# The chunk rows of an SSD scan: a state product from split operands, and dt moved into the exponents

## The chip, the cores and the metric

The kernel runs on one core of a Trainium2 chip. The metric is the device time of one execution in microseconds, of which the median of three runs is given. The core's engines are TensorE (PE in the profile, with its weight loads as PEld), VectorE (DVE), ScalarE (ACT), GpSimd (POOL) and SyncE (SP, which here only starts transfers). Each works through its own queue in order, and they wait for one another with semaphores.

## The reference, cut to what matters

One inference step of a hybrid decoder layer: a pooling branch and a state-space branch side by side, merged by gates. 1024 rows of a prompt and 64 rows of samples go through it. The part that the change touches is the scan of the state-space branch over the prompt. It has 32 heads of 64 channels in 4 groups of 8, a state of 128 by 64 for each head, and goes over the rows in 8 chunks of 128. For each chunk the reference computes:

```
acs = cumsum(dq * A)                       # per row and head
decay[i, j] = exp(acs[i] - acs[j])         # i >= j, else 0
att = (C B^T)[i, j] * decay[i, j] * dq[j]
y = att @ x  +  C (exp(acs) * h)
w_in = exp(last - acs) * dq
h = h * exp(last)  +  B^T (w_in * x)
```

After it y gets d_skip * x added, is multiplied by silu(z), and goes through a norm and an output projection. All of it is float32.

## The kernel before, in words

The large products are done with operands split into two parts (a high part rounded to the type that the program calls F32R, and the rest as a low part), as three matmuls: high by high, high by low, low by high. Products of plain F32 operands go through TensorE in full precision, at more time for each column.

The stages follow one another: the input projection (up to some 480 us), the samples' scan woven into the last input products (to about 750 us), the prompt's chunks (about 757 to 1043 us), and the output products (to the end). `dt_end`, among the samples, makes the small tables that all chunks use: `dtT` (dt by row, chunk and head), `acT` (the running sum of dt times the positive rate, so that decays are exponentials of its negative), `wdT` (w_in) and `Elb` (exp(last)). It also writes the running sums to memory, from where `decays` loads them spread over all partitions.

A chunk, `chunk(g, c)` at L1492, is a generator in five steps, which the loop at L1844 takes at different times:

1. Loads, on SP: the running sums into `dec` (3 buffers), B and C into `bc`, and x into `xb` (5 buffers). Taken three chunks ahead.
2. ACT makes `cE`, the exponential of the running sums (L1504); POOL replaces what lies above the diagonal by a large number (L1229); ACT makes eight exponentials, one for each head, with the head's `acT` as bias (L1233). Two chunks ahead.
3. TensorE transposes x (L1511) and B (L1513) and multiplies B by C (L1514). ACT copies the transposed B to `bt` (L1516), and C into the same PSUM bank (L1518). DVE reads the transposed x from its bank twice: times dt into `xd` (L1522), and times w_in into `xw` (L1524, one buffer). DVE then multiplies `dec` and `cE` by the two products' rows (L1529, L1531). One chunk ahead.
4. TensorE makes the new state's product `pu` from `bt` and `xw` (L1536), and the heads' sums in `inner`: `xd` with `dec` (L1245) and the old state with `cE` (L1248). POOL lets the old state decay (L1542) and DVE adds `pu` (L1544) and d_skip * x (L1548).
5. `finish`, at L1462: times silu(z), which `load_sz` has loaded (3 buffers), split into high and low, and squares summed.

Between these steps the loop takes products of the pooling branch and of the chunks' results (`pieces`, whose matmuls are at L221), 2.56 pieces for each chunk, so that TensorE has work throughout. It also prepares the last products' weights (`wo_splits`, L1766).

What sets the order: over the chunk stage TensorE's and SP's instructions are held in the order in which the program writes them (`in_line`, L202, with ORDER at L1832). The instructions of ACT, DVE and POOL are put in order by the planner of the tile framework, which goes by its own simulated times. Two engines' uses of one PSUM tile are put one behind the other by the framework. PSUM tiles come from three sets: PA (three banks, the woven products), PB (four, with the transposes, the products of B and C, and the heads' sums taking turns) and PC (one, the state's product).

Of the kernel before, what the change touches and what calls it, by code (L numbers as in the profile page):

```python
# [8 lines left out]
F32 = mybir.dt.float32  # L9
F32R = mybir.dt.float32r  # L10
AF = mybir.ActivationFunctionType
ALU = mybir.AluOpType
# [8 lines left out]
P = 128  # L21
# [3 lines left out]
NB = 8  # L25
NS = 64
T = SEQ + NS
DI = 2048
NH = 32
# [4 lines left out]
NC = SEQ // CH  # L34
# [12 lines left out]
def tile_pool_ssd_step(  # L47
# [5 lines left out]
    nc = tc.nc  # L53
    uid = [0]

    def nm(s):
        uid[0] += 1
        return f"{s}_{uid[0]}"
# [25 lines left out]
    right = tc.tile_pool(name="tf", bufs=1, side="right", reuse_waits="tile")  # L84
# [8 lines left out]
    def Y4(pool, dt=F32R):  # L93
        return pool.tile([P, 4, T], dt, tag="Y", name=nm("Y"), bufs=2)

    def PB():
        return psB.tile([P, 512], F32, tag="ps", name=nm("ps"))
# [4 lines left out]
    def PC():  # L102

        return psC.tile([P, 512], F32, tag="pc", name=nm("pc"))
# [6 lines left out]
    mm = nc.tensor.matmul  # L111
    act = nc.scalar.activation
    V = nc.vector
# [990 lines left out]
    def dt_end():  # L1104
# [17 lines left out]
        def tmp(tag, bufs):  # L1122
            return sp.tile([P, 512], F32, tag=tag, name=nm(tag), bufs=bufs)[:, :F]
# [16 lines left out]
        r, e, p = tmp("xd", 2), tmp("xw", 1), tmp("hT", 1)  # L1140
# [18 lines left out]
        dt = dtT.rearrange("p c h -> p (c h)")  # L1159
# [20 lines left out]
        ac = acT.rearrange("p c h -> p (c h)")  # L1180
# [10 lines left out]
        for c0 in (8, 0, 4):  # L1191
            cs = range(c0, min(c0 + 4, 9))
            n = sum(P if c < 8 else NS for c in cs)
            ps = PB()
            for c in cs:
                m = P if c < 8 else NS
                nc.tensor.transpose(ps[:NH, (c - c0) * P:(c - c0) * P + m], acT[:m, c, :], ident[:m, :m])
            if c0 == NC:
                Es[0] = sp.tile([P, 2, 512], F32, tag="h0", name="E", bufs=H0B)[:NH, 0, :NS]
                V.tensor_copy(Es[0], ps[:NH, :n])  # L1200
                store_(acS_d.rearrange("b h t -> h b t"), Es[0].rearrange("h (b t) -> h b t", t=8))
            else:
                at = sp.tile([P, 512], F32, tag="xd", name=nm("at"), bufs=2)[:NH]
                V.tensor_copy(at[:, :n], ps[:NH, :n])
                store_(acs_d[c0:c0 + 4].rearrange("c h t -> h c t"), at.rearrange("h (c t) -> h c t", t=P))

    Es = [None, None]

# [14 lines left out]
    def decays(dec, g, c):  # L1223

        load(dec, acs_d[c, 8 * g:8 * g + 8, :].partition_broadcast(P))

    def far(dec, c):

        nc.gpsimd.affine_select(dec, dec, [[0, 8], [1, P]], ALU.is_ge, FAR, base=0, channel_multiplier=-1)  # L1229

    def exps(dec, g, c):
        for h in range(8):
            act(dec[:, h], dec[:, h], AF.Exp, bias=acT[:, c, 8 * g + h:8 * g + h + 1], scale=-1.0)  # L1233

    def load_E(E2, g):
        for hh in range(2):
# [3 lines left out]
    def inner(xd, dec, S, state=None, cE=None):  # L1240
        pi = PB()
        for q in range(4):
            o = [pi[64 * hh:64 * hh + 64, q * S:(q + 1) * S] for hh in range(2)]
            for hh in range(2):
                mm(o[hh], xd[:S, 2 * q + hh, :], dec[:S, 2 * q + hh], start=True, stop=state is None)  # L1245
            for hh in range(2 if state is not None else 0):
                h = 2 * q + hh
                mm(o[hh], state[:, h * 64:h * 64 + 64], cE[:, h], start=False, stop=True)  # L1248
        return pi[:, :4 * S].rearrange("p (q i) -> p q i", i=S)
# [205 lines left out]
    hst = [None] * NG  # L1455

    CKL = ("sz", "v")

    def ckt(shape, tag, bufs=2):
        return (cl if tag in CKL else ca if tag in ("dec", "xb", "cE", "bc") else ck).tile(list(shape), F32, tag=tag, name=nm(tag), bufs=bufs)  # L1460

    def finish(g, o, S, v, sz, y=None):  # L1462

# [21 lines left out]
    szs = []  # L1485

    def load_sz(j):
        g, c = divmod(j, NC)
        szs.append(ckt([P, 4, P], "sz", 3))
        load(szs[-1], z_d[g][:, :, c * P:c * P + P])  # L1490

    def chunk(g, c):  # L1492
        o = c * P
        dec = ckt([P, 8, P], "dec", 3)
        decays(dec, g, c)
        bc = ckt([P, 2, P], "bc", 3)
        load(bc, xbc_d[g][c][:, 4:6])
        Bf, Cf = bc[:, 0], bc[:, 1]
        xb = ckt([P, 4, P], "xb", 5)
        load(xb, xbc_d[g][c][:, 0:4])  # L1500
        yield
        if c > 0:
            cE = ckt([P, 8, P], "cE")
            act(cE, dec, AF.Exp, scale=-1.0)  # L1504
        if g > 0 or c > 0:
            far(dec, c)
            exps(dec, g, c)
            yield
        px = PB()
        for q in range(4):  # L1510
            nc.tensor.transpose(px[:, q * P:(q + 1) * P], xb[:, q], ident)  # L1511
        pbc = PB()
        nc.tensor.transpose(pbc[:, :P], Bf, ident)  # L1513
        mm(pbc[:, P:2 * P], Bf, Cf, start=True, stop=True)  # L1514
        bt = ckt([P, P], "bt", 2)
        act(bt, pbc[:, :P], AF.Copy)  # L1516
        if c > 0:
            act(pbc[:, 2 * P:3 * P], Cf, AF.Copy)  # L1518
        pxv = px.rearrange("p (h d) -> p h d", d=64)
        heads = slice(8 * g, 8 * g + 8)  # L1520
        xd = ckt([P, 8, 64], "xd", 2)
        V.tensor_tensor(xd, pxv, dtT[:, c, heads].unsqueeze(2).to_broadcast([P, 8, 64]), ALU.mult)  # L1522
        xw = ckt([P, 8, 64], "xw", 1)
        V.tensor_tensor(xw, pxv, wdT[:, c, heads].unsqueeze(2).to_broadcast([P, 8, 64]), ALU.mult)  # L1524
        if g == c == 0:
            yield
            far(dec, c)
            exps(dec, g, c)
        V.tensor_tensor(dec, dec, pbc[:, P:2 * P].unsqueeze(1).to_broadcast([P, 8, P]), ALU.mult)  # L1529
        if c > 0:  # L1530
            V.tensor_tensor(cE, cE, pbc[:, 2 * P:3 * P].unsqueeze(1).to_broadcast([P, 8, P]), ALU.mult)  # L1531
        yield
        if c == 0:
            yh[g], yl[g] = [Y4(hs if g % 2 else hp) for _ in range(2)]
        pu = PC()
        mm(pu, bt, xw.rearrange("p h d -> p (h d)"), start=True, stop=True)  # L1536
        pi = inner(xd, dec, P, *((hst[g], cE) if c > 0 else ()))
        hn = ckt([P, 512], "hst", 2)
        if c == 0:
            act(hn, pu, AF.Copy)  # L1540
        else:
            nc.gpsimd.tensor_tensor(hn.rearrange("p (h d) -> p h d", d=64), hst[g].rearrange("p (h d) -> p h d", d=64),  # L1542
                                    Elb[:, c, heads].unsqueeze(2).to_broadcast([P, 8, 64]), ALU.mult)
            V.tensor_tensor(hn, hn, pu, ALU.add)  # L1544
        hst[g] = hn

        for q in range(4):
            V.scalar_tensor_tensor(pi[:, q], xb[:, q], Dv[:, 4 * g + q:4 * g + q + 1], pi[:, q], ALU.mult, ALU.add)  # L1548
        yield
        finish(g, o, P, xb, szs.pop(0), pi)  # L1550
        if c == NC - 1:
            store_(new_ssm_p[g], hn)
# [55 lines left out]
        gas.append(right.__enter__())  # L1608

    def to_ssd():  # L1610
        nonlocal right, sd, sp, mask, maskS, blkS, dtT, acT, wdT, Elb, ElS
        right.__exit__(None, None, None)
        sd_cm = tc.tile_pool(name="sd", bufs=1, side="right", reuse_waits="tile")
        sd = sd_cm.__enter__()
        right_all.append(sd_cm)

        def one(shape, name):
            return sd.tile(shape, F32, tag=name, name=name, bufs=1)
        mask, maskS, blkS = one([P, P], "mask"), one([NS, NB, 8], "maskS"), one([NS, NS], "blkS")
        dtT, acT, wdT = one([P, 9, NH], "dtT"), one([P, 9, NH], "acT"), one([P, 9, NH], "wdT")  # L1620
        Elb, ElS = one([P, NC, NH], "Elb"), one([P, NB, NH], "ElS")
        right = tc.tile_pool(name="sp", bufs=2, side="right", reuse_waits="tile")
        sp = right.__enter__()
        dt_steps.append(dt_end())
        next(dt_steps[0])
    dt_steps = []
    right_all = []
    sd = sp = mask = maskS = blkS = dtT = acT = wdT = Elb = ElS = None

    first()  # L1630

# [55 lines left out]
    ca = None  # L1687
# [13 lines left out]
    cl = open_("cl", 2)  # L1701
    right = tc.tile_pool(name="ck", bufs=2, side="right", reuse_waits="tile")
    ck = right.__enter__()
    for shape, tag, bufs in (((P, 512), "ph", 3), ((P, P), "bt", 2), ((P, 8, 64), "xd", 2), ((P, 8, 64), "xw", 1),
                             ((P, 4, NS), "szs", 1), ((P, 512), "t2", 1), ((P, 512), "hst", 2)):
        ckt(shape, tag, bufs)

    sq_acc = hs.tile([P, T], F32, tag="sq", name="sq_acc", bufs=1)
# [127 lines left out]
    for _ in range(FRONT - 1):  # L1836
        next(pc_)
    next(seq[0])
    load_sz(0)
    next(seq[1])  # L1840
    next(pc_)
# [271 lines left out]
    for half in range(2):  # L2113
        c = slice(half * 512, half * 512 + 512)
# [168 lines left out]
```

## Time and profile before

| | us |
|---|---|
| three runs, median (lowest to highest) | 1214.07 (1212.27 to 1215.41) |
| the profiled execution | 1210.91 |
| its span | 1209.2 |
| busy: PE | 1194.4 |
| busy: PEld | 1118.5 |
| busy: DVE | 924.8 |
| busy: POOL | 763.4 |
| busy: ACT | 649.1 |

The span reaches from the first to the last instruction of the profiled execution. "Busy" is the time in which an engine had at least one instruction in work; a matmul's duration holds the time until its results are out, so that following matmuls overlap, and what one costs is read from start to start. A row of a group gives the line, the engine, the operation, the tiles (what is written, then what is read), the shapes and the count; behind the first bar the busy time in us and the mean duration in ns; behind the second the idle time of the engine just before, and what it had waited for. Idle time of an engine other than the one that sets the end costs nothing in itself.

### The profile page before, as it was taken

How to read it: one execution, taken by the hardware profiler on the slowest of the kernel's cores; microseconds unless marked ns; L12 is line 12 of the kernel's file. 1: busy time of each engine (PE TensorE's matmuls, PEld its weight loads, DVE VectorE, ACT ScalarE, POOL GpSimd, SP SyncE). 2: the span in 40 equal slices, each digit the busy share in tenths (PEclk: the TensorE clock that was granted, in tenths of full speed). 3: DMA queues.
4: the chain of work that ended last, by engine and by line, in shares of the span. 5: the costliest groups of instructions: out<-in, count | busy, mean ns of one | idle time of the engine just before them, and what ended most of it. 6: DMA issues, size and time to landing. Idle time of an engine off the chain costs nothing.

```text
span 1209.2 us, 25239 instructions
## 1 busy us (share of the span) xinstructions
PE 1194.4 (99%) x9242; PEld 1118.5 (93%) x9242; DVE 924.8 (76%) x1535; ACT 649.1 (54%) x1479; POOL 763.4 (63%) x655
## 2 busy tenths in 40 slices
PE   9999999999999999999999999999999999999997
PEld 8879999999999999999989999988888888999885
DVE  6993788877989578877576555687878889679976
ACT  6864356565666557454434334566676657312435
POOL 1137878875988787764777776255767758423653
PEclk9999999999999999999999999999999999999999
DMA  9836445574556455454667767988879888585794
GB/s 352 306 132 219 136 144 184 164 228 146 171 174 198 160 164 172 135 169 131 208 227 238 245 223 247 320 309 262 270 250 294 277 284 285 173 326 166 235 212 154
DMA packets 167924, 262.72 MB, mean 217 GB/s; under 512 B 32880, under 2 KB 80760, under 8 KB 167800
## 3 DMA queue, kind: packets, MB, share of 16 engines
q1 hardware_dynamic: 90408, 166.01, 41.9%
q10 hardware_dynamic: 73232, 87.16, 21.2%
q0 software_dynamic: 4160, 7.94, 3.2%
q8 instruction: 73, 1.20, 0.4%
q14 instruction: 51, 0.42, 0.1%
HBM read 173.31 MB, written 87.73 MB: 216 GB/s over the span
## 4 chain that ended last, share of the span: by engine, by line
PE 87%; DVE 5%; DMA 3%; ACT 2%; issue 1%; POOL 0%; ACTq 0%; DVEq 0%; SPq 0%; POOLq 0%
PE mm L411 24%; PE ps L411 23%; PE mm L221 17%; PE pc L411 5%; PE ps L1245 3%; PE pc L1536 2%; PE ps L1248 2%; PE ps L2036 2%; PE ps L2034 2%; PE ps L2035 2%; PE ps L1511 1%; DMA dec<-acs_d 1%; DMA Y<-in_x_prompt 1%; PE ps L957 1%; DVE tf L643 1%
## 5 line engine op out<-in xcount | busy, mean ns | idle before, releaser
L148 POOL TENSOR_TENSOR wlo<-rawA,whi 128x512 fp32r<-128x512 f32 x120 | 174.7, 1461 | 80.7 <-ACT whi L145 79.4
L221 PE MATMUL mm<-Y,whi 128*128 128x352 f32 (+1 forms) x960 | 195.9, 334 | 0.8 <-DVE G L1969 0.6
L148 POOL TENSOR_TENSOR wlo<-raw,whi 128x512 fp32r<-128x512 f32 x90 | 149.8, 1673 | 64.6 <-ACT whi L145 62.2
L221 PEld LDWEIGHTS mm<-Y,whi 128*128 128x128 f32 x960 | 159.2, 188 | 7.6 <-issue 4.1
L1089 DVE SCALAR_TENSOR_TENSOR GA<-GA,cvT,GA 128x1112 f32<-128x1112 f32 x72 | 134.0, 1866 | 0.1
L411 PE MATMUL mm<-Y,whi 128*128 128x272 f32 x800 | 118.4, 290 | 0.0
L145 ACT ACTIVATE whi<-rawA 128x512 fp32r<-128x512 f32 x120 | 75.1, 627 | 79.6 <-PE ps L411 34.7
L411 PE MATMUL ps<-Y,whi 128*128 128x272 f32 x800 | 117.4, 289 | 0.0
L145 ACT ACTIVATE whi<-raw 128x512 fp32r<-128x512 f32 x90 | 56.0, 629 | 103.9 <-DVE raw L348 34.0
L411 PEld LDWEIGHTS mm<-Y,whi 128*128 128x128 f32 x800 | 106.9, 188 | 2.5 <-issue 1.0
L411 PEld LDWEIGHTS ps<-Y,whi 128*128 128x128 f32 x800 | 107.0, 188 | 0.8 <-issue 0.7
L221 PE MATMUL mm<-Y,wlo 128*128 128x352 f32 (+1 forms) x480 | 98.5, 327 | 0.0
L1233 ACT ACTIVATE dec<-dec,acT 128x128 f32<-128x128 f32 x256 | 78.8, 389 | 25.8 <-POOL dec L1229 25.8
L221 PEld LDWEIGHTS mm<-Y,wlo 128*128 128x128 f32 x480 | 81.7, 188 | 0.0
L286 POOL TENSOR_TENSOR pw<-pw,ph 128x512 fp32r<-128x512 f32 x40 | 67.0, 1675 | 13.4 <-ACT ph L284 12.5
L1468 POOL TENSOR_TENSOR Y<-xb,Y 128x512 fp32r<-128x512 f32 x32 | 41.2, 1287 | 53.7 <-ACT Y L1466 53.7
L411 PE MATMUL mm<-G,whi 128*128 128x272 f32 x480 | 71.2, 290 | 0.0
L411 PE MATMUL ps<-G,whi 128*128 128x272 f32 x480 | 70.3, 289 | 0.0
L411 PE MATMUL mm<-Y,wlo 128*128 128x272 f32 x400 | 66.8, 288 | 0.0
L411 PE MATMUL ps<-Y,wlo 128*128 128x272 f32 x400 | 66.6, 288 | 0.0
L411 PEld LDWEIGHTS mm<-G,whi 128*128 128x128 f32 x480 | 64.1, 188 | 1.2 <-issue 1.1
L411 PEld LDWEIGHTS ps<-G,whi 128*128 128x128 f32 x480 | 64.2, 188 | 0.3 <-issue 0.3
(579 smaller groups left out, 3130.5 us busy)
## 6 DMA issues: line engine op xcount, KB each, us to landing
rawA<-in_w_in SPq DMA_DIRECT2D x62, 512.0 KB
dec<-acs_d SPq DMA_DIRECT2D x32, 512.0 KB
xbc<-GA ACTq DMA_DIRECT2D x24, 512.0 KB
Y<-wo SPq DMA_DIRECT2D x10, 1024.0 KB
pw<-in_w_ssm_out ACTq DMA_DIRECT2D x32, 256.0 KB
ws<-ph ACTq DMA_DIRECT2D x32, 256.0 KB
ws<-pw ACTq DMA_DIRECT2D x32, 256.0 KB
h<-in_state_ssm SPq DMA_DIRECT2D x32, 256.0 KB
```

Of the source, the lines that this page charges most:

```text
L145: ins = act(hi[:, :, :ncols], raw[:, :, :ncols], AF.Copy)
L148: (eng or nc.gpsimd).tensor_tensor(lo[:, :, :ncols], raw[:, :, :ncols], hi[:, :, :ncols].bitcast(F32), ALU.subtract)
L221: mm(ps[:, :n], w[k // 4][h][:, k % 4, :], r[k][:, o:o + n], start=(j == 0), stop=(j == len(terms) - 1))
L286: nc.gpsimd.tensor_tensor(raw.bitcast(F32R), raw, hi.bitcast(F32), ALU.subtract)
L411: mm(p, w[j // 8][:, k], A(k, s)[j // 4 == 1], start=(j == 0), stop=(j == 11))
L1089: V.scalar_tensor_tensor(d[:, :n], rp[:, k:k + n], cvT[:, 24 * k + mc:24 * k + mc + 1], d[:, :n], ALU.mult, ALU.add)
L1233: act(dec[:, h], dec[:, h], AF.Exp, bias=acT[:, c, 8 * g + h:8 * g + h + 1], scale=-1.0)
L1245: mm(o[hh], xd[:S, 2 * q + hh, :], dec[:S, 2 * q + hh], start=True, stop=state is None)
L1248: mm(o[hh], state[:, h * 64:h * 64 + 64], cE[:, h], start=False, stop=True)
L1468: nc.gpsimd.tensor_tensor(yl[g][:, :, o:o + S], v, yhc.bitcast(F32), ALU.subtract)
L1536: mm(pu, bt, xw.rearrange("p h d -> p (h d)"), start=True, stop=True)
L2034: mm(ps, hi, y[:, k, c0:c0 + cw], start=(first and k == 0), stop=False)
```

## The change

Four things are changed, all in the prompt's chunks or for them.

The state's product is made from split operands. `bt` becomes a pair, its first half rounded by ACT, its second half the rest, by DVE from PSUM. `xw` is split into `xh`, by ACT, and `xl`, by POOL, each with two buffers. Three matmuls add up in `pu` in place of the one in full precision.

dt goes into the exponents. `dt_end` makes a new table `alT` = ln(max(dt, 1e-37)) + running sum, for the chunks. The eight exponentials take it as bias in place of `acT`, so that the decays come out multiplied by dt. `xd` is then the transposed x as it is, and ACT copies it from PSUM; before, DVE multiplied it there.

There are more buffers: four for `sz`, six for `xb`.

The order of the tiles in the pool that opens for the chunks is another, with `xh` and `xl` among them, and the copy of C into PSUM (L1518 before) is written behind the two readings of the transposed x.

```diff
+        al = alT.rearrange("p c h -> p (c h)")
+        V.tensor_scalar(al, dt[:, :256], 1e-37, None, ALU.max)
+        act(al, al, AF.Ln)
+        V.tensor_tensor(al, al, ac[:, :256], ALU.add)
...
-            act(dec[:, h], dec[:, h], AF.Exp, bias=acT[:, c, 8 * g + h:8 * g + h + 1], scale=-1.0)
+            act(dec[:, h], dec[:, h], AF.Exp, bias=alT[:, c, 8 * g + h:8 * g + h + 1], scale=-1.0)
...
-        szs.append(ckt([P, 4, P], "sz", 3))
+        szs.append(ckt([P, 4, P], "sz", 4))
...
-        xb = ckt([P, 4, P], "xb", 5)
+        xb = ckt([P, 4, P], "xb", 6)
...
-        bt = ckt([P, P], "bt", 2)
-        act(bt, pbc[:, :P], AF.Copy)
-        if c > 0:
-            act(pbc[:, 2 * P:3 * P], Cf, AF.Copy)
+        bt = ckt([P, 2, P], "bt", 2, F32R)
+        act(bt[:, 0], pbc[:, :P], AF.Copy)
...
-        V.tensor_tensor(xd, pxv, dtT[:, c, heads].unsqueeze(2).to_broadcast([P, 8, 64]), ALU.mult)
-        xw = ckt([P, 8, 64], "xw", 1)
-        V.tensor_tensor(xw, pxv, wdT[:, c, heads].unsqueeze(2).to_broadcast([P, 8, 64]), ALU.mult)
+        act(xd, pxv, AF.Copy)
+        xw, xh, xl = ckt([P, 512], "xw", 1), ckt([P, 512], "xh", 2, F32R), ckt([P, 512], "xl", 2, F32R)
+        V.tensor_tensor(xw.rearrange("p (h d) -> p h d", d=64), pxv,
+                        wdT[:, c, heads].unsqueeze(2).to_broadcast([P, 8, 64]), ALU.mult)
+        if c > 0:
+            act(pbc[:, 2 * P:3 * P], Cf, AF.Copy)
+        act(xh, xw, AF.Copy)
+        nc.gpsimd.tensor_tensor(xl, xw, xh.bitcast(F32), ALU.subtract)
...
+        V.tensor_tensor(bt[:, 1], pbc[:, :P], bt[:, 0].bitcast(F32), ALU.subtract)
...
-        mm(pu, bt, xw.rearrange("p h d -> p (h d)"), start=True, stop=True)
+        mm(pu, bt[:, 0], xh, start=True, stop=False)
+        mm(pu, bt[:, 1], xh, start=False, stop=False)
+        mm(pu, bt[:, 0], xl, start=False, stop=True)
...
-    for shape, tag, bufs in (((P, 512), "ph", 3), ((P, P), "bt", 2), ((P, 8, 64), "xd", 2), ((P, 8, 64), "xw", 1),
-                             ((P, 4, NS), "szs", 1), ((P, 512), "t2", 1), ((P, 512), "hst", 2)):
+    for shape, tag, bufs in (((P, 8, 64), "xd", 2), ((P, 2, P), "bt", 2), ((P, 512), "ph", 3), ((P, 4, NS), "szs", 1), ((P, 512), "t2", 1),
+                             ((P, 512), "hst", 2), ((P, 512), "xw", 1), ((P, 512), "xh", 2), ((P, 512), "xl", 2)):
```

More of the change, by code (lines that the diff above doesn't have):

```diff
@@ L1457, in tile_pool_ssd_step, with ckt @@
     CKL = ("sz", "v")
-    def ckt(shape, tag, bufs=2):
-        return (cl if tag in CKL else ca if tag in ("dec", "xb", "cE", "bc") else ck).tile(list(shape), F32, tag=tag, name=nm(tag), bufs=bufs)
+    def ckt(shape, tag, bufs=2, dt=F32):
+        return (cl if tag in CKL else ca if tag in ("dec", "xb", "cE", "bc") else ck).tile(list(shape), dt, tag=tag, name=nm(tag), bufs=bufs)
     def finish(g, o, S, v, sz, y=None):
@@ L1610, in to_ssd @@
     def to_ssd():
-        nonlocal right, sd, sp, mask, maskS, blkS, dtT, acT, wdT, Elb, ElS
+        nonlocal right, sd, sp, mask, maskS, blkS, dtT, acT, wdT, alT, Elb, ElS
         right.__exit__(None, None, None)
@@ L1620, in to_ssd @@
         dtT, acT, wdT = one([P, 9, NH], "dtT"), one([P, 9, NH], "acT"), one([P, 9, NH], "wdT")
-        Elb, ElS = one([P, NC, NH], "Elb"), one([P, NB, NH], "ElS")
+        alT, Elb, ElS = one([P, NC, NH], "alT"), one([P, NC, NH], "Elb"), one([P, NB, NH], "ElS")
         right = tc.tile_pool(name="sp", bufs=2, side="right", reuse_waits="tile")
@@ L1627, in tile_pool_ssd_step @@
     right_all = []
-    sd = sp = mask = maskS = blkS = dtT = acT = wdT = Elb = ElS = None
+    sd = sp = mask = maskS = blkS = dtT = acT = wdT = alT = Elb = ElS = None
     first()
```

## The prediction

> **What bounds the kernel now.** I first read the page: span, busy time per engine, and the engine line of the chain that ended last.
>
> ```profile
> span 1209.2 us, 25239 instructions
> ...
> PE 1194.4 (99%) x9242; PEld 1118.5 (93%) x9242; DVE 924.8 (76%) x1535; ACT 649.1 (54%) x1479; POOL 763.4 (63%) x655
> ...
> PE 87%; DVE 5%; DMA 3%; ACT 2%; issue 1%; POOL 0%; ACTq 0%; DVEq 0%; SPq 0%; POOLq 0%
> ```
>
> TensorE is busy for 99% of the span, but an average may hide a stage with another limit, so I then read busy times over 27 stretches of 10 us from 770 to 1040 us, which is where the chunks run (three stretches and the sum here), and TensorE's own list of waits from 750 to 1050 us.
>
> ```profile
> 870.00:880.00 10.00, 10.00 (x81) 9.05 (x80) 7.77 (x15) 7.43 (x19) 10.00 (x12) 1.00 0.76 228
> ...
> 910.00:920.00 10.00, 10.00 (x84) 8.99 (x85) 7.72 (x14) 8.09 (x22) 10.00 (x11) 1.00 0.98 305
> ...
> 1000.00:1010.00 10.00, 10.00 (x81) 9.05 (x81) 9.93 (x19) 5.61 (x12) 10.00 (x12) 1.00 0.81 264
> ...
> sum 270.00, PE 269.53 PEld 239.46 DVE 223.11 ACT 167.28 POOL 177.32; mean PE 9.98 PEld 8.87 DVE 8.26 ACT 6.20 POOL 6.57
> ```
>
> ```profile
> PE ps L1513 <- DVE cE L1531: 0.3, 1, 0.3
> PE mm L221 <- DVE Y L1567: 0.2, 1, 0.2
> ```
>
> The columns after the stretch are its length, then PE, PEld, DVE, ACT and POOL busy, the granted clock (1.00), the DMA share and GB/s. In 270 us TensorE is without work for 0.5 us, and all its waits in 300 us are those two, 0.5 us. So here a microsecond of matmul taken away is a microsecond of span, and a microsecond added to another engine is free as long as TensorE never has to wait for it. POOL fills the three stretches shown, and DVE nearly fills the last: those are the places where this could fail.
>
> **The change part by part. First the state's product (L1536), the only TensorE work that changes.** The timeline of TensorE around one of them:
>
> ```profile
> 900.73 0.81 PE L221 MATMUL mm<-Y,whi 128*128 128x352 f32 x4
> 901.38 1.02 PE L1536 MATMUL pc<-xw,bt 128*128 128x512 f32 x2
> 902.33 0.44 PE L1245 MATMUL ps<-dec,xd 128*64 128x128 f32 x4
> ```
>
> Durations include the drain of a pipelined matmul, so I count from start to start: 902.33 - 901.38 = 0.95 us for the full-precision product (two records). The new one is three matmuls of 128x512 on split operands. The kernel already has these, in the last products, where hi.hi, hi.lo and lo.hi follow each other with a new stationary operand each time:
>
> ```profile
> 1122.04 0.40 PE L2034 MATMUL ps<-Y,a11h 128*128 128x512 f32 x1
> 1122.27 0.40 PE L2035 MATMUL ps<-Y,a11h 128*128 128x512 f32 x1
> ...
> 1123.44 0.40 PE L2034 MATMUL ps<-Y,a11h 128*128 128x512 f32 x1
> ```
>
> From the first to the last are six intervals in 1.40 us, 0.233 us each, so three take 0.70 us. But 0.95 also holds the passage to L1245, whose tiles are 128*64. What that costs after split operands, a place among the samples shows:
>
> ```profile
> 583.42 0.66 PE L411 MATMUL mm<-G,wlo 128*128 128x272 f32 x4
> 583.91 1.16 PE L411 MATMUL ps<-G,whi 128*128 128x272 f32 x8
> ...
> 584.92 0.67 PE L411 MATMUL ps<-G,wlo 128*128 128x272 f32 x4
> 585.51 0.68 PE L1245 MATMUL ps<-dec,xd 64*64 64x64 f32 x16
> ```
>
> Four matmuls take 0.49 us when their own kind follows, 0.59 us when L1245 follows: 0.10 us for the passage. New slot: 0.70 + 0.10 = 0.80 us, saving 0.15 us. There are 32 chunks (64 records of L1536 in pairs): **32 x 0.15 = 4.8 us less**. Upper bound: no passage, 32 x 0.25 = 8.0 us less. Lower bound: the weight loads, 188 ns each by their group in this stage,
>
> ```profile
> L1536 PEld LDWEIGHTS pc<-xw,bt 128*128 128x128 f32 x64 | 11.3, 188 | 0.0
> ```
>
> not hidden: 3 x (0.233 + 0.188) + 0.10 = 1.36 us, 32 x 0.41 = 13 us more. The L2034 rows, each with a load of its own, speak for the hidden case; I take 4.8.
>
> The Trainium skill's page "TensorE: Matmul & The Clock Gate" (section on NX overlap, "why back-to-back is faster than the latency suggests") gives 216 ns from one 512-column matmul to the next; the rows here show 233 ns. By the page the slot would be 0.65 + 0.10 and the gain, by that estimate, 6.4 us; the rows are of this kernel's own operands and decide.
>
> **The vector work of a chunk.** The groups of instructions between 750 and 1050 us, and one of the page (L148):
>
> ```profile
> L1468 POOL TENSOR_TENSOR Y<-xb,Y 128x512 fp32r<-128x512 f32 x32 | 41.2, 1287 | 53.7 <-ACT Y L1466 53.7
> L1548 DVE SCALAR_TENSOR_TENSOR ps<-xb,Dv,ps 128x128 f32<-128x128 f32 x128 | 44.8, 350 | 4.5 <-PE ps L1248 2.4
> L1529 DVE TENSOR_TENSOR dec<-dec,ps 128x1024 f32<-128x1024 f32 x32 | 38.9, 1216 | 24.6 <-ACT ps L1518 6.4 <-POOL sq_acc L1475 4.9 <-POOL sq_acc L1472 3.3
> L1524 DVE TENSOR_TENSOR xw<-ps,wdT 128x512 f32<-128x512 f32 x32 | 21.9, 683 | 4.9 <-PE pc L1536 4.8
> L1522 DVE TENSOR_TENSOR xd<-ps,dtT 128x512 f32<-128x512 f32 x32 | 21.8, 680 | 0.8 <-PE ps L1511 0.8
> L1466 ACT ACTIVATE Y<-xb 128x512 fp32r<-128x512 f32 x32 | 19.9, 623 | 20.8 <-DVE xb L1464 20.8
> L1540 ACT ACTIVATE hst<-pc 128x512 f32<-128x512 f32 x4 | 2.3, 585 | 2.6 <-PE pc L1536 2.6
> ```
>
> ```profile
> L148 POOL TENSOR_TENSOR wlo<-raw,whi 128x512 fp32r<-128x512 f32 x90 | 149.8, 1673 | 64.6 <-ACT whi L145 62.2
> ```
>
> DVE loses the scaled xd (0.68) and gains the low half of bt, 128x128 with one operand in PSUM, between a quarter of xw's 683 ns (0.17) and L1548's 0.35; nearest in size and place is L1548, so 0.35: net -0.33 us a chunk, 32 x 0.33 = 11 of 223 us. ACT gains the plain copy of xd out of PSUM (L1540, 0.585) and xh (L1466, 0.623): 1.21 us a chunk, 39 us, 167 to 206 of 270. POOL gains xl: 1.29 (L1468) to 1.67 us (L148 with another neighbour), 41 to 54 us, 177 to 218-231 of 270. None exceeds 86% of the stage, and TensorE's 270 us of work covers all; so zero on the end. Without that cover the new chain xd, xw, xh, xl is 0.59 + 0.68 + 0.62 + 1.29 = 3.2 us, paid as far as it overruns its time. That time the timeline shows:
>
> ```profile
> 898.68 0.60 PE L1511 MATMUL ps<-ident,xb 128*128 128x128 f32 x4
> ...
> 900.06 1.06 ACT L1504 ACTIVATE cE<-dec 128x1024 f32<-128x1024 f32 x1 [2.75 <-DMA dec<-acs_d]
> ...
> 902.43 0.27 ACT L1516 ACTIVATE bt<-ps 128x128 f32<-128x128 f32 x1
> ...
> 905.11 0.68 DVE L1524 TENSOR_TENSOR xw<-ps,wdT 128x512 f32<-128x512 f32 x1
> ...
> 906.69 0.27 PE L1513 MATMUL ps<-ident,bc 128*128 128x128 f32 x1
> ...
> 909.11 1.02 PE L1536 MATMUL pc<-xw,bt 128*128 128x512 f32 x2
> ```
>
> The transposes of a chunk end at 899.3, its state product starts at 909.1: 9.8 us for a chain of 3.2 us, even here, where ACT stood 2.75 us for a late decay and bt came at 902.4. The new first step, xd, is queued on ACT behind bt, hence about 902.7 to 903.3; xw then to 904.0, xh near 905, xl near 907 if POOL is free. About 2 us are left. The second limit is the PSUM bank of px, which (of four) the second transposes after it take, at 906.69 here. Before, xw held it until 905.79, because xw has one buffer and its predecessor is read by the fp32 product (4.8 us of waiting); now xw's buffer is freed by xh and xl, so that wait goes and the bank should not be held longer. What is late next is xl, on POOL, behind whatever POOL waits for in order (53.7 us behind L1466).
>
> **More buffers, and the one-off part.** The loads' queue waits:
>
> ```profile
> SPq L1225 <- PE ps L1248: 89.6, 24, 5.8
> ...
> SPq L1490 <- POOL sq_acc L1475: 8.8, 4, 2.5
> ```
>
> A fourth sz buffer and a sixth xb one remove waits like the second (8.8 us over 300 us); the decays' wait, ten times larger, stays. TensorE waits for no load, so: nothing. The new alT is made once among the samples: three DVE operations and one logarithm on 128x256, with a table load or two:
>
> ```profile
> L1186 DVE TENSOR_TENSOR wdT<-wdT,dtT x2: 174/292/410, 566.0 to 566.3; 128x256 f32<-128x256 f32 x1, 64x32 f32<-64x32 f32 x1
> ...
> L1185 ACT ACT_TABLE_LOAD  x1: 1283/1283/1283, 563.8 to 563.8; - x1
> ```
>
> ```profile
> 560.00:600.00 40.00, 40.00 (x323) 37.72 (x322) 20.90 (x42) 21.87 (x45) 24.83 (x23) 1.00 0.56 181
> ```
>
> Two DVE operations at 0.41, an ACT one of about the same, up to two loads at 1.28: 3.8 us at most. TensorE is full there and DVE and ACT half idle, and the first use is in the chunks' stage: nothing, 3.8 us if that cover failed. The exponentials only change their bias; the heads' sums keep their shapes.
>
> **Sum.** -4.8 + 0 + 0 + 0. The profiled execution took 1210.91 us (1.7 us around its span of 1209.2), so it would become 1206.1; it lies 3.2 us below the median of the three runs, 1214.07. Against the median: **1209.3 us**.
>
> **Rivals.**
> 1. *Taken up again by late operands.* In the POOL-full stretches (870-880, 910-920 and 1000-1010 us) xl comes after its 2 us of room. For: POOL at 10.00 there, and 1.3 to 1.7 us more for each chunk. Against: POOL's mean of 6.57, and what it does besides in a chunk is mostly needed later. About four chunks touched by 1 us each: 4.8 - 4 leaves 1213.
> 2. *The shared bank (other side).* px, so far read by DVE alone, is now read by ACT and then by DVE. That two engines reading one bank are put one behind the other, L1529 shows: it waited 6.4 us for L1518, which touches other columns of the same bank. So xw, at the head of DVE's queue, waits for ACT whenever ACT stands for a decay, and behind xw stand the products with the decays, the state's sum and the additions of the woven products' results, which TensorE needs next. It decides once ACT is some 2 us later than at 902.4 above. If that costs half a microsecond in each of 32 chunks: +16 - 4.8 = 1225. Against: ACT is idle 38% of the stage, and DVE already waited for ACT here without TensorE waiting. The Trainium skill, "PSUM - Partial Sum Buffer", section on bank collisions, says the same of any two engines on one bank and quadrant, readers included; by that rule this wait must exist, and the trace agrees with its 6.4 us.
> 3. *No cheaper product* (the change doesn't do what it says): loads not hidden, +13, 1227. The L2034 rows speak against it.
> 4. *More than forecast*: no passage, 8.0 less, 1206.
>
> **How the numbers follow.** Forecast 0.60, rival 1 0.18, rival 2 0.12, rival 3 0.03, rival 4 0.07. About 0.3% (3.6 us: below 1210.4, above 1217.7) is what can be told from no change here. The three runs spread over 3.1 us, so from the forecast I count 0.47 of its 0.60 as faster and 0.13 as the same; with rival 4, faster 0.54; with rival 1, same 0.31; rivals 2 and 3, slower 0.15. Range: down to 1205 (rival 4 and a microsecond of scatter), up to 1219, which takes in rival 1 and the milder half of rival 2. The forecast's own range is 1206 to 1212.
>
> **What would show it.** Right: L1536 in three groups of 32 and 0.80 us from its first start to L1245; TensorE's waits in the stage still under 2 us; DVE some 11 us less busy, ACT some 39 and POOL 41 to 54 us more; the chunks' stage nearly 5 us shorter and the rest as it was. Wrong: new rows under TensorE's waits, on xl or xh (rival 1), or on xd, xw, dec or hst with DVE waiting for ACT's copy of xd (rival 2); a slot over 0.95 us (rival 3).

## The result, and the profile after

The change made the kernel slower by 0.24%: the median is 1215.28 us against 1212.1 us for the kernel before in the same comparison, a ratio of 1.0024 with a 95% interval of 1.0014 to 1.0033. The forecast was 1209.3 us. The medians of the kernel before in the comparisons here lie between 1212.1 and 1214.1 us, so everything below is told as a ratio to the kernel before on the same chip, or from single profiled executions.

First the page of the kernel after: the span, the busy times, and the engine line of the chain that ended last.

```profile
span 1212.2 us, 25452 instructions
...
PE 1190.9 (98%) x9274; PEld 1125.4 (93%) x9274; DVE 917.6 (76%) x1537; ACT 680.5 (56%) x1545; POOL 802.9 (66%) x687
...
PE 76%; DVE 8%; DMA 6%; ACT 5%; issue 2%; POOL 2%; SPq 1%; ACTq 0%; DVEq 0%; POOLq 0%
```

TensorE has less to do, 1190.9 us where it had 1194.4, and yet the span is 3.0 us longer; its share of the last chain fell from 87% to 76%. The timeline shows two of the new state products. The first runs as planned:

```profile
988.76 0.39 PE L1544 MATMUL pc<-xh,bt 128*128 128x512 f32 x1
988.99 0.40 PE L1545 MATMUL pc<-xh,bt 128*128 128x512 f32 x1
989.22 0.40 PE L1546 MATMUL pc<-xl,bt 128*128 128x512 f32 x1
989.55 0.44 PE L1249 MATMUL ps<-dec,xd 128*64 128x128 f32 x4
```

From 988.76 to 989.55 are 0.79 us, for 0.95 before. 26 of the 32 products take 0.78 to 0.80 us. The second is one of the other six:

```profile
1005.67 0.39 PE L1544 MATMUL pc<-xh,bt 128*128 128x512 f32 x1
1005.90 0.40 PE L1545 MATMUL pc<-xh,bt 128*128 128x512 f32 x1
...
1007.70 0.50 PE L1546 MATMUL pc<-xl,bt 128*128 128x512 f32 x1 [1.40 <-POOL xl L1531]
1008.13 0.44 PE L1249 MATMUL ps<-dec,xd 128*64 128x128 f32 x4
```

Its slot is 2.46 us. The six slots are 2.82, 2.76, 1.05, 2.25, 2.46 and 2.18 us, together 8.8 us above six times 0.79. The list of TensorE's waits from 770 to 1045 us names what was late:

```profile
PE pc L1546 <- POOL xl L1531: 4.1, 4, 1.4
PE ps L1249 <- ACT G L1747: 1.6, 1, 1.6
PE ps L1249 <- DVE cE L1539: 1.0, 1, 1.0
PE ps L1252 <- DVE cE L1539: 0.6, 1, 0.6
PE ps L1249 <- ACT xd L1524: 0.2, 1, 0.2
```

The heads' sums (L1249) do not read G, so what released them in the second row stays open. The rows sum to 7.5 us; 6.9 of it lies in the slots (the 0.6 before L1252 comes behind one), while the slots grew by 8.8. In the late product above the row says 1.40 us and the slot grew by 1.67: the row counts from the end of the matmul before (1005.90 + 0.40), while in the product that ran as planned the next matmul starts 0.17 us before that end, and the late matmul stands 0.43 us ahead of the next in place of 0.33. So the stage as a whole lost. From the first state product to the last it was 268.42 us before:

```profile
772.10 1.02 PE L1536 MATMUL pc<-xw,bt 128*128 128x512 f32 x2
...
1040.52 1.02 PE L1536 MATMUL pc<-xw,bt 128*128 128x512 f32 x2
```

and is 272.13 us after:

```profile
770.77 0.39 PE L1544 MATMUL pc<-xh,bt 128*128 128x512 f32 x1
...
1042.90 0.39 PE L1544 MATMUL pc<-xh,bt 128*128 128x512 f32 x1
```

That is +3.7 us: 32 x 0.16 = 5.1 us gained, 8.8 us lost in six chunks. The other engines' new work is close to what was forecast: by the two pages DVE is busy 7.2 us less than before (11 forecast), ACT 31.4 us more (39) and POOL 39.5 us more (41 to 54). The groups from 750 to 1050 us:

```profile
L1531 POOL TENSOR_TENSOR xl<-xw,xh 128x512 fp32r<-128x512 f32 x32 | 41.8, 1305 | 28.9 <-ACT xh L1530 28.9
...
L1526 DVE TENSOR_TENSOR xw<-ps,wdT 128x512 f32<-128x512 f32 x32 | 22.0, 688 | 20.7 <-ACT xd L1524 19.7 <-POOL xl L1531 1.0
L1530 ACT ACTIVATE xh<-xw 128x512 fp32r<-128x512 f32 x32 | 19.9, 623 | 6.9 <-DVE xw L1526 6.5 <-ACT ph L1781 0.4
...
L1524 ACT ACTIVATE xd<-ps 128x512 f32<-128x512 f32 x32 | 18.8, 588 | 8.8 <-PE ps L1515 8.8
...
L1536 DVE TENSOR_TENSOR bt<-ps,bt 128x128 fp32r<-128x128 f32 x32 | 9.1, 286 | 10.1 <-ACT ps L1529 10.1
```

The durations (1305, 623, 588 and 286 ns) are close to the estimates. What was not in the estimate is the last column: DVE stood 19.7 us before xw for ACT's copy of xd, which reads the same PSUM bank, and 10.1 us before the low half of bt for ACT's copy of C. Before, xw waited 4.9 us in all, and for C's copy DVE waited 6.4 us, before dec. The chain of the late product above, read from the timeline (rows of TensorE and of the other engines):

```profile
993.48 0.60 PE L1515 MATMUL ps<-ident,xb 128*128 128x128 f32 x4
```

```profile
996.32 0.57 ACT L1524 ACTIVATE xd<-ps 128x512 f32<-128x512 f32 x1
...
997.51 0.68 DVE L1526 TENSOR_TENSOR xw<-ps,wdT 128x512 f32<-128x512 f32 x1
...
1001.58 0.62 ACT L1530 ACTIVATE xh<-xw 128x512 fp32r<-128x512 f32 x1
...
1006.38 1.26 POOL L1531 TENSOR_TENSOR xl<-xw,xh 128x512 fp32r<-128x512 f32 x1
```

The transposes end at 994.08. xd comes 2.2 us later on ACT, xw 0.6 us after it, xh 3.4 us after that on ACT again, xl 4.2 us after that on POOL: 3.1 us of work (0.57 + 0.68 + 0.62 + 1.26) over 13.6 us, of which 10.4 are queues. TensorE waited for xl in three other chunks. In the one at 932.8 us ACT came to xd 6.0 us after the transposes; in the one at 969.2 the queues took 2.5 us before xd, 1.6 before xw, 1.9 before xh and 2.5 before xl; in the one at 1014.9 xh began as soon as xw was there, and POOL came to xl 6.3 us later.

### The profile page after: what moved, and what is told of

It is laid out like the page before. It is cut to its first block, busy times and chain, and to the rows that moved or that the text cites. A ratio compares the mean times of both kernels' runs of the same rounds, so it can differ in the third digit from the quotient of the medians.

```text
span 1212.2 us, 25452 instructions
## 1 busy us (share of the span) xinstructions
PE 1190.9 (98%) x9274; PEld 1125.4 (93%) x9274; DVE 917.6 (76%) x1537; ACT 680.5 (56%) x1545; POOL 802.9 (66%) x687
## 4 chain that ended last, share of the span: by engine, by line
PE 76%; DVE 8%; DMA 6%; ACT 5%; issue 2%; POOL 2%; SPq 1%; ACTq 0%; DVEq 0%; POOLq 0%
PE mm L411 24%; PE ps L411 24%; PE mm L221 11%; PE pc L411 5%; PE ps L1249 2%; DMA dec<-acs_d 1%; PE ps L1252 1%; DMA v<-ys 1%; DMA R<-in_w_o 1%; PE ps L2046 1%; PE ps L2045 1%; PE ps L2044 1%; ACT dec L1237 1%; DMA Y<-in_x_prompt 1%; PE ps L957 1%
## 5 line engine op out<-in xcount | busy, mean ns | idle before, releaser
L1237 ACT ACTIVATE dec<-dec,alT 128x128 f32<-128x128 f32 x256 | 78.6, 391 | 8.0 <-POOL dec L1233 8.0
L1531 POOL TENSOR_TENSOR xl<-xw,xh 128x512 fp32r<-128x512 f32 x32 | 41.8, 1305 | 28.9 <-ACT xh L1530 28.9
```

Of the source, the lines that this page charges most:

```text
L1237: act(dec[:, h], dec[:, h], AF.Exp, bias=alT[:, c, 8 * g + h:8 * g + h + 1], scale=-1.0)
L1531: nc.gpsimd.tensor_tensor(xl, xw, xh.bitcast(F32), ALU.subtract)
```

## The experiments

In each the kernel after is edited, and timed against the kernel before. Theory A was that POOL comes to xl too late. Theory B was that ACT's copy of xd makes what follows late, because DVE's xw must read the same bank after it and stands at the head of DVE's queue. Theory C came later: that ACT has too much work.

No edit changes one thing alone: the planner sets the order of ACT's, DVE's and POOL's instructions anew for each kernel, and the traces show other orders. Where such an order bears on a reading, it is told there.

| kernel | ratio to before (95%) | first to last state product, us |
|---|---|---|
| before | 1 | 268.4 |
| the change | 1.0024 (1.0014 to 1.0033) | 272.1 |
| split product alone | 0.9981 (0.9970 to 0.9992) | 266.8 |
| dt in the exponents alone | 1.0037 (1.0023 to 1.0052) | 270.2 |
| xl on DVE | 1.0074 (1.0058 to 1.0090) | 275.5 |
| xd copied by DVE | 0.9994 (0.9983 to 1.0005) | 267.2 |
| xw ahead of xd | 1.0008 (0.9994 to 1.0022) | 269.2 |
| priority for xh and xl | 1.0030 (1.0018 to 1.0043) | 273.1 |
| split alone, C's copy early | 0.9987 (0.9973 to 1.0000) | 267.5 |
| split alone, old buffers | 0.9986 (0.9974 to 0.9997) | 266.6 |
| 8 columns read by ACT first | 1.0066 (1.0049 to 1.0083) | 274.6 |
| idle copy on ACT | 1.0028 (1.0016 to 1.0041) | 269.7 |
| split alone, xw ahead of xd | 0.9999 (0.9988 to 1.0010) | 266.5 |
| split alone, high parts only | 0.9950 (0.9933 to 0.9968) | 262.5 |

The last column is of one execution each; the ratio also holds what happens before the first product and after the last.

**The split product alone.**

```diff
-        al = alT.rearrange("p c h -> p (c h)")
-        V.tensor_scalar(al, dt[:, :256], 1e-37, None, ALU.max)
-        act(al, al, AF.Ln)
-        V.tensor_tensor(al, al, ac[:, :256], ALU.add)
...
-            act(dec[:, h], dec[:, h], AF.Exp, bias=alT[:, c, 8 * g + h:8 * g + h + 1], scale=-1.0)
+            act(dec[:, h], dec[:, h], AF.Exp, bias=acT[:, c, 8 * g + h:8 * g + h + 1], scale=-1.0)
...
-        act(xd, pxv, AF.Copy)
+        V.tensor_tensor(xd, pxv, dtT[:, c, heads].unsqueeze(2).to_broadcast([P, 8, 64]), ALU.mult)
```

> The state's product from split operands and the larger buffers stay; dt goes back out of the exponents, so that DVE again makes xd times dt and ACT has no copy of xd. Theory A (POOL reaches xl too late): TensorE's waits on xl stay, some 4 us or more, and the time stays near that of the whole change, 1.002 of before. Theory B (ACT's copy of xd in front of DVE's reading of the same bank makes the whole chain late): the waits go, the cheaper slot of 0.79 us is left, 0.996 of before.

Measured 0.9981: faster than before, and 0.43% under the whole change. TensorE's waits from 770 to 1045 us in this kernel:

```profile
PE ps L1513 <- DVE xb L1464: 1.8, 1, 1.8
PE ps L1245 <- ACT G L1743: 0.9, 1, 0.9
PE ps L1248 <- DVE cE L1535: 0.6, 1, 0.6
PE ps L1245 <- ACT bt L1516: 0.3, 1, 0.3
```

No wait on xl is left, though POOL makes it as before; and DVE, with more work than in the whole change, is no longer in the way. So POOL's work alone does not make xl late. Its order may: in the 28th and 29th chunk (at 1005.7 and 1014.9 us in the whole change) POOL came to xl 4.2 and 6.3 us after xh, and here it comes after 1.8 and 2.5 us. The expectation of theory B, 0.996, was not reached either: some 3.6 us of waits on other things remain. The longest can be followed back:

```profile
950.20 2.97 POOL L1779 TENSOR_TENSOR R<-R,ph 128x512 fp32r<-128x512 f32 x2
...
954.25 2.46 ACT L1233 ACTIVATE dec<-dec,acT 128x128 f32<-128x128 f32 x8 [1.54 <-POOL dec L1229]
...
957.95 0.68 DVE L1464 TENSOR_TENSOR xb<-ps,sz 128x512 f32<-128x512 f32 x1
...
958.69 0.33 PE L1513 MATMUL ps<-ident,bc 128*128 128x128 f32 x1 [1.83 <-DVE xb L1464]
```

POOL split weights for the last products until 953.17 and came only then to the mask of the decays (L1229). ACT waited 1.54 us for it with eight exponentials, which end at 956.71. DVE's product of the decays starts at 956.81, and the end of an old chunk (L1464) stands behind it. So POOL's queue reaches TensorE by another way than xl, too.

**dt in the exponents alone.**

```diff
-        bt = ckt([P, 2, P], "bt", 2, F32R)
-        act(bt[:, 0], pbc[:, :P], AF.Copy)
+        bt = ckt([P, P], "bt", 2)
+        act(bt, pbc[:, :P], AF.Copy)
...
-        act(xh, xw, AF.Copy)
-        nc.gpsimd.tensor_tensor(xl, xw, xh.bitcast(F32), ALU.subtract)
...
-        V.tensor_tensor(bt[:, 1], pbc[:, :P], bt[:, 0].bitcast(F32), ALU.subtract)
...
-        mm(pu, bt[:, 0], xh, start=True, stop=False)
-        mm(pu, bt[:, 1], xh, start=False, stop=False)
-        mm(pu, bt[:, 0], xl, start=False, stop=True)
+        mm(pu, bt, xw, start=True, stop=True)
```

> dt in the exponents, ACT's copy of xd and the larger buffers stay; the state's product goes back to one full-precision matmul, so xh, xl and the low half of bt are not made. Theory A: no xl, no waits; the slot is 0.95 us again, 1.000 of before within 0.002. Theory B: TensorE still waits for what stands behind xd, 3 us or more, 1.003 of before or above.

Measured 1.0037, the number of theory B: slower without any xl. But of the 5.9 us between this profiled execution and that of the kernel before, only 1.8 lie in the stage; the first state product starts 4.1 us later (776.21 for 772.10). The timeline of the first chunk shows what happened there:

```profile
765.80 0.28 ACT L1520 ACTIVATE bt<-ps 128x128 f32<-128x128 f32 x1 [6.48 <-DMA gs<-u]
765.97 0.59 ACT L1524 ACTIVATE xd<-ps 128x512 f32<-128x512 f32 x1
...
766.59 0.69 DVE L1526 TENSOR_TENSOR xw<-ps,wdT 128x512 f32<-128x512 f32 x1 [5.33 <-ACT xd L1524]
767.20 1.41 DVE L1724 TENSOR_TENSOR R<-mm,R 128x384 f32<-128x384 f32 x3
...
767.80 0.97 PE L221 MATMUL mm<-Y,whi 128*128 128x384 f32 x4 [2.21 <-DVE R L1724]
```

ACT waited 6.48 us for a transfer that had nothing to do with x. DVE, which had all that it needed but the bank, waited 5.33 us for ACT's copy with xw at the head of its queue. Behind xw stood the results of the woven products (L1724), and TensorE waited 2.21 us for one of their banks. The whole change has no such wait there, and why this kernel has it was not traced. So most of this kernel's loss lies ahead of the stage, and its number is weak support for theory B; what is shown is how a delay of ACT reaches TensorE.

**xl on DVE.**

```diff
-        nc.gpsimd.tensor_tensor(xl, xw, xh.bitcast(F32), ALU.subtract)
+        V.tensor_tensor(xl, xw, xh.bitcast(F32), ALU.subtract)
```

> As the whole change, but DVE makes xl in place of POOL: some 0.7 to 0.95 us more on DVE for each chunk, 1.3 us less on POOL. Theory A: the waits on xl go, about 4 us less than the whole change, 0.998 to 0.999 of before, if DVE, which is fullest from 950 us on, does not become late itself. Theory B: as the whole change or slower, 1.002 to 1.005.

Measured 1.0074, worse than either theory's number. TensorE's waits (770 to 1045 us) still have xl first, now by DVE, and DVE's own first wait is that of the whole change (19.7 us there):

```profile
PE pc L1546 <- DVE xl L1531: 5.8, 3, 2.5
```

```profile
DVE xw L1526 <- ACT xd L1524: 20.8, 14, 3.6
```

Taking 1.3 us a chunk off POOL did not help. But the step went to DVE, busy 227.8 of the 270 us from 770 us on in this kernel (POOL 183.1), and now DVE makes xl late, so the run does not decide about theory A.

**xd copied by DVE.**

```diff
-        act(xd, pxv, AF.Copy)
+        V.tensor_copy(xd, pxv)
```

> As the whole change, but DVE copies xd out of PSUM in place of ACT, so that one engine reads that bank, as before the change; DVE has 0.68 us more for each chunk and ACT 0.59 less. Theory A: the waits on xl stay, 1.002 of before. Theory B: they go, 0.996 to 0.997.

Measured 0.9994. With this one line TensorE's waits on xl are gone and 0.30% of the whole change's time with them; theory B's 0.996 is again not reached. POOL, with the same work, comes to xl sooner here as well, 2.2 and 2.6 us after xh in the 28th and 29th chunk. Against the split alone (0.9981) the intervals overlap, so what dt in the exponents costs or brings by itself, with xd on the same engine, is not resolved.

**xw ahead of xd.**

```diff
-        act(xd, pxv, AF.Copy)
...
         V.tensor_tensor(xw.rearrange("p (h d) -> p h d", d=64), pxv,
                         wdT[:, c, heads].unsqueeze(2).to_broadcast([P, 8, 64]), ALU.mult)
+        act(xd, pxv, AF.Copy)
```

> As the whole change, but DVE's xw is written ahead of ACT's copy of xd, so that DVE reads the transposed x as soon as it is there and ACT reads the bank after it. The two engines still share the bank and do the same work. Theory B (xw at the head of DVE's queue waits for ACT): DVE's 19.7 us of waiting before xw goes, with it most of TensorE's waits; 0.997 to 0.999 of before. If ACT's added work in itself is too much (theory C): the waits move to xd and the heads' sums, 1.001 to 1.003.

Measured 1.0008. DVE no longer waits before xw, and one of four waits on xl is left (1.5 us); waits on the decays' products (2.0 us) and others stay. The value lies between theory B and theory C. It is 0.16% under the whole change, but the two intervals overlap, so this gain is not clear of the scatter.

**Priority for xh and xl.**

```diff
+        with tc.high_priority():
-        act(xh, xw, AF.Copy)
-        nc.gpsimd.tensor_tensor(xl, xw, xh.bitcast(F32), ALU.subtract)
+            act(xh, xw, AF.Copy)
+            nc.gpsimd.tensor_tensor(xl, xw, xh.bitcast(F32), ALU.subtract)
```

> As the whole change, but xh and xl have high priority with the planner, so that ACT and POOL take them earlier in their queues. Theory B: xw is still late, so little changes: 1.001 to 1.003, while waits on the decays' products stay. If only the place of xl in POOL's queue matters (theory A): TensorE's 4.1 us of waiting for xl go, 0.998 to 0.999.

Measured 1.0030, with 4.0 us of waits on xl as in the whole change. The priority did not move what it was meant to move: in the 28th and 29th chunk POOL still comes to xl 4.5 and 6.2 us after xh. So theory A was not tested by it.

**The split alone, with C's copy early, and with the old buffers.**

```diff
         act(bt[:, 0], pbc[:, :P], AF.Copy)
+        if c > 0:
+            act(pbc[:, 2 * P:3 * P], Cf, AF.Copy)
...
-        if c > 0:
-            act(pbc[:, 2 * P:3 * P], Cf, AF.Copy)
         act(xh, xw, AF.Copy)
```

> The split product alone (dt out of the exponents, xd on DVE as before, larger buffers), and C's copy into PSUM written right behind the copy of bt, as before the change. Theory B's second half (the low half of bt and the decays' products wait for this copy because it comes last on ACT): DVE's 9.3 us of waiting for it go to below 4, and the 3.7 us of stalls that the split alone still has shrink to 2 or less; 0.996 to 0.997 of before. If its place does not matter: 0.998 as the split alone.

```diff
-        szs.append(ckt([P, 4, P], "sz", 4))
+        szs.append(ckt([P, 4, P], "sz", 3))
...
-        xb = ckt([P, 4, P], "xb", 6)
+        xb = ckt([P, 4, P], "xb", 5)
```

> The split product alone, with three buffers for sz and five for xb as before. If the buffers do nothing: 0.998 as the split alone with the larger ones. If they matter: 1.000 or above, with SyncE waiting longer for the ends of old chunks and TensorE for loads.

Measured 0.9987 and 0.9986: neither differs from the split alone. DVE still waits 8.0 us for C's copy, so its place in the program decides little, and the buffers do nothing that can be measured.

**Bank or work: eight columns read by ACT first, and an idle copy on ACT.** Both start from the kernel in which DVE copies xd (0.9994).

```diff
-        act(xd, pxv, AF.Copy)
+        act(ckt([P, 8], "jk", 1), px[:, 0:8], AF.Copy)
+        V.tensor_copy(xd, pxv)
```

> The whole change with xd copied by DVE, and in front of that a copy by ACT of 8 columns of the transposed x, whose result nothing uses: hardly any work for ACT, but the bank is again read by ACT first and by DVE after it. Theory B (DVE's queue stands until ACT has read the bank): DVE waits some 15 to 20 us for that copy and TensorE gets its waits back, 1.001 to 1.003 of before. Theory C (it is ACT's added work that counts): as with xd on DVE alone, 0.999 to 1.000.

```diff
-        act(xd, pxv, AF.Copy)
+        V.tensor_copy(xd, pxv)
+        act(ckt([P, 512], "jk", 1, mybir.dt.bfloat16), xb.rearrange("p q t -> p (q t)"), AF.Copy)
```

> The whole change with xd copied by DVE, and a copy by ACT of the loaded x (128x512, from SBUF to SBUF) in each chunk, whose result nothing uses: ACT has the work of the change, but the bank of the transposed x is read by DVE alone. Theory B: as with xd on DVE alone, 0.999 to 1.000 of before. Theory C: 1.002 to 1.003, as the whole change.

The read of eight columns gave 1.0066, 0.72% more than without it. TensorE's waits and DVE's first wait in this kernel:

```profile
PE pc L1547 <- POOL xl L1532: 6.3, 4, 3.8
PE ps L1249 <- DVE cE L1540: 1.0, 2, 0.5
```

```profile
DVE xd L1525 <- ACT jk L1524: 14.1, 9, 3.5
```

A tiny instruction on ACT, put in front of DVE's reading of the bank, brings the waits on xl back (6.3 us), as theory B has it. But it is not only DVE's waiting that does it. 3.8 of the 6.3 us belong to one chunk, the 28th:

```profile
1003.71 0.68 DVE L1525 COPY xd<-ps 128x512 f32<-128x512 f32 x1
...
1005.16 0.62 ACT L1531 ACTIVATE xh<-xw 128x512 fp32r<-128x512 f32 x1
...
1006.95 1.06 POOL L1553 TENSOR_TENSOR hst<-hst,Elb 128x512 f32<-128x512 f32 x1
...
1011.39 1.28 POOL L1532 TENSOR_TENSOR xl<-xw,xh 128x512 fp32r<-128x512 f32 x1
```

DVE did not wait before this xd, which comes 7.0 us after the transposes, and POOL, never idle, comes to xl 5.6 us after xh, behind the old state's decay (hst) and more. In the same chunk of the kernel without the eight columns xl stands ahead of that decay, 2.2 us after xh:

```profile
1003.02 1.30 POOL L1531 TENSOR_TENSOR xl<-xw,xh 128x512 fp32r<-128x512 f32 x1
...
1004.28 1.04 POOL L1552 TENSOR_TENSOR hst<-hst,Elb 128x512 f32<-128x512 f32 x1
```

So the eight columns came with another order of the queues, and how much each of the two cost stays open. The idle copy gave 1.0028, so ACT's time counts as well, with no bank shared. That run is not clean either: ACT's queue also stood 19.3 us for the loads of x at the head of that copy:

```profile
ACT jk L1525 <- DMA xb<-xbc: 19.3, 12, 2.8
```

So the work, this wait or another order of the queues did it. How the loss that comes with ACT's copy divides between the shared bank, ACT's work and the planner's order stays open.

**The split alone, with xw ahead of xd.** The same exchange in the kernel with the split product only, where DVE does both.

```diff
-        V.tensor_tensor(xd, pxv, dtT[:, c, heads].unsqueeze(2).to_broadcast([P, 8, 64]), ALU.mult)
...
         V.tensor_tensor(xw.rearrange("p (h d) -> p h d", d=64), pxv,
                         wdT[:, c, heads].unsqueeze(2).to_broadcast([P, 8, 64]), ALU.mult)
+        V.tensor_tensor(xd, pxv, dtT[:, c, heads].unsqueeze(2).to_broadcast([P, 8, 64]), ALU.mult)
```

> The split product alone (dt out of the exponents, xd times dt on DVE), with xw written ahead of xd on DVE. If the chain xw, xh, xl is still the longest way to the state's product: 0.997 of before, a little under the split alone. If the stalls that the split alone has left (about 3.7 us, none of them on xl) are of the decays' products and the banks: 0.998, no change.

Measured 0.9999, above both expected values: no wait on xl, as before, and 1.1 us on a decays' product whose operand DVE makes behind these steps. The stage is as long as in the split alone (266.5 and 266.8 us), so what made the whole slower lies outside it or in the scatter. The chain to xl is not what the split alone still waits for.

**The split alone, high parts only.**

```diff
-        nc.gpsimd.tensor_tensor(xl, xw, xh.bitcast(F32), ALU.subtract)
...
-        V.tensor_tensor(bt[:, 1], pbc[:, :P], bt[:, 0].bitcast(F32), ALU.subtract)
...
-        mm(pu, bt[:, 1], xh, start=False, stop=False)
-        mm(pu, bt[:, 0], xl, start=False, stop=True)
+        mm(pu, bt[:, 0], xh, start=False, stop=False)
+        mm(pu, bt[:, 0], xh, start=False, stop=True)
```

> TensorE's side of the split product alone: dt is out of the exponents, xd times dt is on DVE, and the three matmuls of the state's product all take the high parts of bt and xw; the low parts are not made and not used, so that the state is not the reference's. TensorE has the slot of 0.79 us, ACT only xh more than before, POOL nothing more, DVE as before. If a microsecond less on TensorE is a microsecond less in the end as long as no operand is late: 32 x 0.16 = 5.1 us less, 0.996 of before, and stalls under 1 us. If the stage has another bound near by (transfers, DVE): 0.998 as the split product, with stalls of some 3 us.

This kernel leaves out the low parts, so its state is not the reference's; it shows only times. Measured 0.9950: the whole gain of TensorE's shorter slot arrives. From 770 to 1040 us TensorE is never idle, in the row of that stretch (PE, PEld, DVE, ACT, POOL busy):

```profile
770.00:1040.00 270.00, 270.00 (x2248) 250.73 (x2247) 227.72 (x383) 188.51 (x484) 183.31 (x210) 1.00 0.86 282
```

The same row of the split alone, with both low parts made:

```profile
770.00:1040.00 270.00, 266.32 (x2214) 246.62 (x2214) 233.33 (x409) 186.52 (x476) 219.18 (x237) 1.00 0.85 277
```

5.6 us more on DVE and 36 us more on POOL, neither of them near 270, cost 3.7 us of TensorE's time and 0.31% of the whole.

## Why the prediction was wrong

**What bounds the kernel: right.** A microsecond off TensorE is a microsecond off the span as long as no operand is late; the kernel with high parts only shows it, with 6.0 us less in the stage and 0.5% less in all.

**The state's product: right.** 0.80 us was forecast and 0.79 measured, in 26 of 32 chunks, and the passage to the heads' sums cost its 0.10 us. The three matmuls stand 0.23 us apart, as in the kernel's own rows and not 216 ns apart as the Trainium skill's page "TensorE: Matmul & The Clock Gate" has it (section on NX overlap). Rivals 3 and 4 are out.

**"So zero on the end": this step failed.** The vector work was costed at nothing, because no engine exceeded 86% of the stage and because one chain had 2 us to spare. Its durations were right. But the sum of an engine's work says nothing about when a chain that goes ACT, DVE, ACT, POOL comes through four queues. The chain that I read, and placed its new steps in by hand, was one in which ACT was late by 2.75 us, and I took that for a bad case; in the late chunk shown above queues alone took 10.4 us. The term that was set to 0 is 8.8 us, all in six chunks between 871 and 1018 us, where POOL is fullest (busy 86% of 870 to 1020 us, 70% of the 100 us before).

The timeline that I read had such a queue in it already. I let xw run from 903.3 to 904.0 and took its one buffer for what had held it. But the product that read this buffer had ended at 902.40; xw started only at 905.11 because DVE was at other work:

```profile
902.80 1.22 DVE L1529 TENSOR_TENSOR dec<-dec,ps 128x1024 f32<-128x1024 f32 x1 [2.79 <-POOL sq_acc L1475]
903.94 1.25 DVE L1793 TENSOR_TENSOR R<-R,R 128x512 f32<-128x512 f32 x1
```

The runs divide the loss. From the high parts only (0.9950) to the split alone (0.9981) are 0.31%: the low parts, on POOL and DVE. From there to the whole change (1.0024) are 0.43%: dt in the exponents, of which 0.30% come back when DVE copies xd. So each of the two groups of steps that were put at nothing cost part of it.

**"The bank should not be held longer": wrong in its reason.** The wait of xw for its one buffer (4.8 us) did go, as forecast, to 1.0 us. In its place came 19.7 us of waiting for ACT's copy of xd. I had counted ACT's 0.59 us, and not that it turns DVE's first step, which had depended on TensorE alone, into one that depends on ACT.

**Rival 2 named a mechanism that is there, and rival 1 the place.** DVE waited 19.7 us for ACT's copy of xd, and 14.1 us for ACT's eight columns. That is the rule of the Trainium skill's page "PSUM — Partial Sum Buffer" (section on bank collisions), that readers of one bank on two engines have to be put one behind the other; both waits agree with it. The row that I took for it before (6.4 us for L1518) was of a reader behind a writer, as L1518 writes C into the bank. POOL's lateness, rival 1's reason, is there as well: 4.2 and 6.3 us before xl in two of the four chunks that waited for it. But rival 2's price of half a microsecond in every chunk was wrong in kind: 26 chunks paid nothing, and six paid 0.3 to 2.0 us. Rival 1 had six late chunks nearly right (four) and each at too little (1 us). I gave the two 0.30 together; as both act on one chain, they should have been one case with a larger chance.

**The buffers and alT: right.** Without the added buffers the split alone is the same within its interval. alT cost one table load (1.28 us) and one logarithm (0.42 us) on ACT among the samples, with nothing seen of it in TensorE's waits there.

The run shows a version that beats both: the split product alone, at 0.9981 of before. It keeps about 0.2% of the 0.5% that TensorE's side offers. Of what the rest of it waits for (3.6 us in all) the longest wait, 1.8 us, goes back to POOL's queue as shown; the others were not traced.

## What to carry to other kernels

When the bounding engine gets cheaper work in exchange for more steps elsewhere, the sum of those steps is the wrong test: follow the chain through every queue that it crosses, in the stretches where these queues are fullest, and ask of each first step whom it waited for before and whom it waits for now. Moving a PSUM read from one engine to another is not only so many nanoseconds on the other engine; a second engine on the same bank ties two queues together, and a stall of one, for whatever reason, then stands at the head of the other. Where a planner orders the queues, an edit of one line can move others, so compare the orders before a difference is put down to that line. Where a change has two parts, the one that pays should be timed alone.

## What was not expected

A read of eight columns (128x8) by ACT, with a result that nothing uses, came with 0.72% more time (1.0066 against 0.9994), by its place in front of DVE's reads of the same bank and the order of the queues that the planner made of it. And a wait costs TensorE more than its row shows: the six late slots grew by 8.8 us, the waits in them sum to 6.9.
